# One group of heads fewer in the plain part of the fifth stage, with the first chunk's sums made behind its norm

## The chip, the cores and the metric

The kernel runs on one core of one Trainium2 chip. Its engines work side by side, each through its own list of instructions in order: TensorE (PE) multiplies matrices, VectorE (DVE) and ScalarE (ACT) work element by element, GpSimd (POOL) and SyncE (SP) mostly start transfers between the chip's buffer and the memory outside it. An engine waits where an instruction needs what another has not finished. The metric is device time in microseconds (us) from start to end of one execution. The kernel before took 2325.74 us, the median of three runs (2324.58 to 2327.02).

## What is computed

A decoder of two layers, 1024 prompt tokens and 8 sampled tokens, width 2048, all in float32. In the reference, cut to what matters here:

```python
# layer A
z = x @ w_in;  u, gate = z[..., :2048], z[..., 2048:]
d = multiscale_pool(u);  d = grouped_linear(d) * scale
h = layer_norm(ALPHA * x + (d * silu(gate)) @ w_out)
# one K and V for what follows
k, v = split(h @ w_kv);  k = rope_partial(k)
# layer B
z = h @ w_in_b;  q = rope_partial(z[..., :2048]);  gate = z[..., 2048:]
o = sliding_window_attention(q, k, v, sinks)      # 32 heads, window 128
y = layer_norm(ALPHA * h + (o * silu(gate)) @ w_out_b)
```

`layer_norm` takes mean and variance over the 2048 channels of a token. The kernel also returns the pooling state and the last keys and values.

## The kernel before, in words

**Chunks and stages.** Channels lie on the 128 partitions, tokens along a row. The tokens are cut into two chunks: chunk 0 has 512 columns, chunk 1 has 520 (512 prompt tokens and the 8 sampled ones). `PHASES` lists ten stages in order: `ai` (layer A's input product, pooling, gate), `ao` (its output product), `bi` (layer B's input product: first K and V, then queries and gates of the heads, and the attention), `bo` (its output product). Counted by kind and chunk, with a stage's two parts taken together, they are ai 0, ai 1, ao 0, ao 1, bi 0 (the fifth), bi 1, bo 0, bo 1.

**Two ways to multiply.** A weight block is 128 partitions by 1024 columns. Each float32 operand is split in a high and a low part (`cast_to` on ACT, line 502; `prep_to` on DVE, line 517), and a product is three matmuls: high by high, high by low, low by high. The plain way (`unit`, lines 709 to 711) needs four weight blocks for a two-by-two set of tiles and runs over all 512 columns. The Strassen way (`seven`, lines 681 to 683) does the same with seven products of half the columns. It needs sums of weight blocks (made on DVE, either by `plain_pair`, line 289, or by `first_pair`, line 347, and stored by POOL for the second chunk, which loads them with `next_pair`) and sums of the activation tiles: `t_ops` (lines 849 to 852) makes four sums of each pair of tiles and stores them in the tensors `Td`, from where `x_load` fetches them.

**Groups of heads.** `bi` works through eight groups p = 0 to 7, each with two query tiles and two gate tiles, so two calls of `attend`. In the plain part a group is four units; in the Strassen part it is two times seven blocks. `PHASES` says how many groups of chunk 0 are plain: `("bi", 0, (0, 3))`, that is p = 0, 1 and 2. `FORM` lists the groups whose weight sums are not made in chunk 0's plain part but in chunk 1 (`bi` 1) with `first_pair`; a plain group outside `FORM` makes and stores them on the way (`plain_pair`).

**The norms run beside the products.** `ln_gen` is a generator: each step issues a few instructions. `end()` runs at the end of each block (of each half block in the plain part) and takes a step of the first generator in the list `side` where a counter says so: one step in `every` ends, if at least `room` buffer slots are free. Extra steps are put at given ends with `at`. Before a stage's activations are first needed, `x_begin` calls `ready`, which takes at once whatever steps of the generator it depends on are left.

- In ao 1 the generator is the norm of chunk 0 (`ln_gen(0, ...)`), one step in two ends (`every = 2`). Given no `td`, its last loop takes one step a pair of tiles: subtract the mean (line 1022), multiply (1023), then on ACT the affine part of the pair before (1014) and its store by SP (1015).
- In the plain part of bi 0 the generators are the norm of chunk 1 (given `td`, so it also calls `t_ops`, two steps a pair) and behind it `t_gen(("h", 0))`, which loads chunk 0's normalised tiles again, makes their sums and stores them. One step is taken at each end, and ten extra steps at the third end and every second one from there. The Strassen part waits in `x_begin` for all of `t_gen`.
- `sum_gen("wob")` makes weight sums for `bo`. It may load while `self.on` is set: from the fourth to the twelfth end of this part, and again from the eighth of bi 1.

**Attention.** `attend` puts the scores on PE (line 1817) nine ends after the unit that makes the queries is begun. The rotated query comes from DVE (`q_done`, lines 1679 and 1787). The softmax runs on ACT and DVE over the next ends (1838, 1842), then come the transposes on PE, a masked copy on DVE (1880) and the product with the values (1894).

Program order is kept on PE, DVE and ACT (`in_order`). PE runs through its blocks; DVE and ACT prepare blocks up to three and four ahead (`self.ahead`), and loads run seven ahead (five in the plain part).

Of the kernel before, what the change touches and what calls it, by code (L numbers as in the profile page):

```python
# [43 lines left out]
C_SCALE, C_GA, C_BA, C_GB, C_BB, C_SINK, C_SDEC = 0, 16, 32, 48, 64, 80, 112  # L44
# [3 lines left out]
N_CST = K_MP + P + 1  # L48

PHASES = (  # L50
    ("ai", 0, (0, 1)), ("ai", 0, (1, 8)), ("ai", 1, (0, 8)), ("ao", 0, None), ("ao", 1, None), ("bi", 0, (0, 3)),
    ("bi", 0, (3, 8)), ("bi", 1, (0, 8)), ("bo", 0, None), ("bo", 1, None),
)
PHASE_OF = {"x": "ai", "g": "ao", "h": "bi", "o": "bo"}
INPUT_OF = {k: x for x, k in PHASE_OF.items()}
# [15 lines left out]
)  # L71

LATE = (2, 3)
FORM = (1, 2,)
X_KEEP = 5
X_AGE = 3
SIDE_KEEP = 5
# [111 lines left out]
class Kern:  # L189
# [1970 lines left out]
    def run(self):  # L2160
# [10 lines left out]
        def add(key, gen):  # L2171
            self.needs.append((key, gen))
            self.side.append(gen)

        acc, before = {}, False
        for n, (kind, c, part) in enumerate(PHASES):
            self.c, self.ph = c, kind + str(c)
            self.strassen = (kind, c, part) not in PLAIN
            self.shared = False
            self.fresh = c == 1 and before and self.strassen  # L2180
            before = c == 0 and self.strassen
            nxt = n + 1 if n + 1 < len(PHASES) else None
            self.every, self.room = 3, SIDE_KEEP
            if n == 0 or (kind, c) == ("bi", 0) and self.wide:
                self.use_four(kind == "ai")
            elif (kind, c) == ("bo", 0):
                self.at(18, lambda: self.use_four(True))

            self.lock = (kind, c) in LOCKED
            self.need = {  # L2190
                (idx, g): self.i + (2 * n + g - 1 if self.lock else n)
                for n, idx in enumerate(ORDERL if self.lock else ORDER7) for g in range(2)
            } if self.strassen else {}
            self.turn = not self.lock
            self.at(7, lambda: setattr(self, "turn", False))
            self.at(13, lambda: setattr(self, "lock", False))
            if n == 0:
                self.at(10, lambda: self.x_begin(1))
                self.at(10, lambda: setattr(self, "turn", True))
            elif (kind, c) == ("ai", 0):  # L2200
                add(("x", 1, False), self.t_gen(("x", 1)))
                self.room = 99
            elif (kind, c) == ("ai", 1):
                add(("g", 0, False), self.t_gen(("g", 0)))
                self.summed["woa"] = 0
                add("woa", self.sum_gen("woa"))
                self.every = 1.7
            elif (kind, c) == ("ao", 0):
                self.every = 2
                self.at(1, lambda: self.nc.sync.dma_start(self.cst[:, K_MP:], io["mask"]))  # L2210
            elif (kind, c) == ("ao", 1):
                gen = self.ln_gen(0, *acc[0], C_GA, C_BA, self.act["h", 0], None)
                self.at(3, lambda gen=gen: add(("h", 0, True), gen))
                self.every = 2
            elif (kind, c) == ("bi", 0) and not self.strassen:
                self.summed["wob"] = 0
                self.extra = self.sum_gen("wob")
                for k in (4, 12):
                    self.at(k, lambda k=k: setattr(self, "on", k == 4))
                add(("h", 1, False), self.ln_gen(1, *acc[1], C_GA, C_BA, self.act["h", 1], self.Td.get(("h", 1))))  # L2220
                add(("h", 0, False), self.t_gen(("h", 0)))

                for k in range(10):
                    self.at(2 * k + 3, lambda: self.side and self.lastO < self.i - 1 and self.side_step())
                self.every = 1
            elif (kind, c) == ("bi", 1):
                self.at(8, lambda: setattr(self, "on", True))
                self.every, self.room = 1, 0
            elif (kind, c) == ("bo", 0):
                self.at(23, lambda: setattr(self, "ahead", (7, 4, 3)))  # L2230
                self.at(18, lambda: add(("o", 1, False), self.t_gen(("o", 1))))
                self.at(16, lambda: [s.free() for s in self.kv])
                self.rt.free()
            elif (kind, c) == ("bo", 1):
                gen = self.ln_gen(0, *acc[0], C_GB, C_BB, io["y0"], None)
                self.at(3, lambda gen=gen: add("y", gen))
                self.every, self.room = 2.75, 3
            if kind == "ai":
                self.phase_ai(c, range(*part), nxt)
            elif kind == "bi":  # L2240
                self.phase_bi(c, range(*part), nxt)
            else:
                res = self.act["x" if kind == "ao" else "h", c]
                last = (C_GB, C_BB, io["y1"]) if nxt is None else None
                acc[c] = self.phase_out(c, res, nxt, last)
# [143 lines left out]
```

## Time and profile before

| | |
|---|---|
| median of three runs | 2325.74 us |
| the profiled execution | 2326.46 us, of which the traced span is 2324.7 us |
| PE busy | 2290.2 us (99% of the span) |
| DVE busy | 1935.0 us (83%) |
| ACT busy | 1381.8 us (59%) |
| moved by transfers | 652.50 MB, 281 GB/s on average |
| ao 1 | about 915 to 1076 us of the span |
| bi 0, plain part | 1076.45 to 1276.75 us |
| bi 0, Strassen part | from 1276.75 us |

The page gives busy time by engine, the span in 40 slices, the transfer queues, the chain that ended last and the costliest groups of instructions. A busy matmul record is longer than the distance to the next one, because matmuls are pipelined: what a stage costs PE is read from the starts of its instructions. Idle time of an engine that is not the bound costs nothing.

### The profile page before, as it was taken

Reading aid. Unit: us, or ns where it says so; the run is one execution under the profiler, and the core shown is the slowest. Engines: PE = TensorE matmul, PEld = TensorE weight load, DVE = VectorE, ACT = ScalarE, POOL = GpSimd, SP = SyncE. Lnnn points to the kernel's source line nnn. Section 1 sums busy time; section 2 is a strip of 40 time slices with the busy share of each in tenths; the row PEclk is TensorE's granted clock in tenths of the full one; section 3 lists DMA queues with packets and bytes.
Section 4 is the critical chain, followed back from the end, with each engine's and each line's share of the span. In section 5 each row is a group of like instructions: output and inputs, shape, how many; then the busy total and the mean of one; then the engine's idle time right before and its main releaser. Section 6 shows DMA issues by size and latency. Waiting matters only on the chain. (4 is left out here: it accounts for less than half of the span.)

```text
span 2324.7 us, 50174 instructions
## 1 busy us (share of the span) xinstructions
PE 2290.2 (99%) x20248; PEld 2208.9 (95%) x20248; DVE 1935.0 (83%) x2398; ACT 1381.8 (59%) x2531; POOL 191.7 (8%) x360
## 2 busy tenths in 40 slices
PE   8999999999999999999999999999999999999997
PEld 6999999999999999999778999999999999999997
DVE  7888889877878878878987888988987777898897
ACT  5554446544546556655466676785676678656565
POOL 0111110010000000000110111100000000000001
PEclk9999999999999999999999999999999999999999
DMA  6868679988889989898797667788586778799794
GB/s 247 280 252 304 234 243 333 322 299 302 303 306 317 338 284 336 321 350 310 236 349 256 220 224 254 256 306 259 178 262 225 252 233 284 254 368 363 266 345 157
DMA packets 247417, 652.50 MB, mean 281 GB/s; under 512 B 25328, under 2 KB 106128, under 8 KB 247184
## 3 DMA queue, kind: packets, MB, share of 16 engines
q1 hardware_dynamic: 205168, 496.81, 63.6%
q0 software_dynamic: 42016, 152.49, 17.0%
q8 instruction: 158, 2.59, 0.4%
q14 instruction: 75, 0.61, 0.1%
HBM read 466.68 MB, written 173.01 MB: 275 GB/s over the span
## 5 line engine op out<-in xcount | busy, mean ns | idle before, releaser
L681 PE MATMUL pD<-m,m 128*128 128x260 f32 (+1 forms) x4976 | 1408.7, 283 | 3.0 <-ACT pD L620 1.3
L683 PE MATMUL pD<-m,m 128*128 128x260 f32 (+1 forms) x4976 | 1402.2, 282 | 6.1 <-DVE m L517 5.7
L682 PE MATMUL pD<-m,m 128*128 128x260 f32 (+1 forms) x4976 | 1402.3, 282 | 0.0
L681 PEld LDWEIGHTS pD<-m,m 128*128 128x128 f32 x4976 | 936.6, 188 | 12.4 <-issue 6.0
L683 PEld LDWEIGHTS pD<-m,m 128*128 128x128 f32 x4976 | 937.7, 188 | 9.2 <-DVE m L517 9.2
L682 PEld LDWEIGHTS pD<-m,m 128*128 128x128 f32 x4976 | 937.0, 188 | 0.5
L517 DVE TENSOR_TENSOR m<-m,m 128x1024 fp32r<-128x1024 f32 x686 | 829.5, 1219 | 93.8 <-ACT m L502 53.8
L502 ACT CAST m<-m 128x1024 fp32r<-128x1024 f32 x686 | 716.9, 1050 | 237.7 <-DVE m L347 116.4
L347 DVE TENSOR_TENSOR m<-m,m 128x1024 f32<-128x1024 f32 x128 | 156.5, 1222 | 8.0 <-DMA m<-in_wia 3.8
L801 DVE TENSOR_TENSOR m<-m,m 128x1024 fp32r<-128x1024 f32 (+1 forms) x120 | 146.3, 1225 | 8.2 <-ACT m L792 4.0
L709 PE MATMUL pD<-m,m 128*128 128x512 f32 x320 | 128.7, 402 | 8.1 <-ACT m L792 8.1
L792 ACT CAST m<-m 128x1024 fp32r<-128x1024 f32 (+1 forms) x120 | 125.5, 1053 | 15.4 <-DVE m L517 4.8
L710 PE MATMUL pD<-m,m 128*128 128x512 f32 x320 | 127.2, 398 | 0.5 <-DVE m L801 0.5
L711 PE MATMUL pD<-m,m 128*128 128x512 f32 x320 | 126.8, 396 | 0.0
L654 ACT COPY m<-pD 128x260 f32<-128x260 f32 (+1 forms) x87 | 32.6, 374 | 128.8 <-PE pD L683 128.6
L642 DVE TENSOR_TENSOR m<-pD,m 128x260 f32<-128x260 f32 (+1 forms) x90 | 37.7, 419 | 76.7 <-ACT pD L641 70.8
L1853 ACT ACTIVATE m<-m,sm 128x128 f32<-128x128 f32 x256 | 99.8, 394 | 0.0
L1128 PE MATMUL pD<-m,m 128*128 128x260 f32 (+1 forms) x528 | 91.2, 323 | 0.0
L620 ACT ACTIVATE pD<-pD 128x260 f32<-128x260 f32 (+1 forms) x88 | 32.7, 371 | 98.3 <-PE pD L683 98.0
L1866 ACT ACTIVATE m<-m,sm 128x128 f32<-128x128 f32 x256 | 82.2, 394 | 12.2 <-DVE sm L1861 11.7
L1128 PEld LDWEIGHTS pD<-m,m 128*128 128x128 f32 x528 | 79.3, 188 | 8.0
L709 PEld LDWEIGHTS pD<-m,m 128*128 128x128 f32 x320 | 60.8, 190 | 23.4 <-ACT m L792 8.1
(247 smaller groups left out, 2065.0 us busy)
## 6 DMA issues: line engine op xcount, KB each, us to landing
m<-in_wia SPq DMA_DIRECT2D x130, 512.0 KB
m<-in_wib SPq DMA_DIRECT2D x130, 512.0 KB
m<-swoa SPq DMA_DIRECT2D x64, 512.0 KB
swia<-m POOLq DMA_DIRECT2D x56, 512.0 KB, 4.9
m<-swia SPq DMA_DIRECT2D x56, 512.0 KB
m<-swob SPq DMA_DIRECT2D x56, 512.0 KB
m<-in_wob SPq DMA_DIRECT2D x52, 512.0 KB
m<-in_woa SPq DMA_DIRECT2D x48, 512.0 KB
```

The source lines that it names most:

```text
L347: self.nc.vector.tensor_add(s[out].a[:, :1024], s[x].a[:, :1024], s[y].a[:, :1024])
L502: self.nc.scalar.copy(hi.r[:, :1024], self.stream[self.cast].src().a[:, :1024])
L517: self.nc.vector.tensor_sub(lo.r[:, :1024], s.src().a[:, :1024], hi.a[:, :1024])
L681: nc.tensor.matmul(ps[:, :TH], wh[:, s], h, start=new and k == 0, stop=False, skip_group_check=on)
L682: nc.tensor.matmul(ps[:, :TH], wh[:, s], l, start=False, stop=False, skip_group_check=on)
L683: nc.tensor.matmul(ps[:, :TH], wl[:, s], h, start=False, stop=k == 7, skip_group_check=on)
L709: nc.tensor.matmul(ps[:], wh[:, s], h, start=par == 0 and k == 0, stop=False)
L710: nc.tensor.matmul(ps[:], wh[:, s], l, start=False, stop=False)
L711: nc.tensor.matmul(ps[:], wl[:, s], h, start=False, stop=par == 1 and k == 7)
L792: self.nc.scalar.copy(h.r[:, :n], s.a[:, :n])
L801: self.nc.vector.tensor_sub(l.r[:, :n], s.a[:, :n], h.a[:, :n])
L1128: nc.tensor.matmul(ps[:, : cs.stop - cs.start], ws[:, s], d[:, cs], start=f0 and k == 0, stop=l0 and k == 3,)
```

## The change

It touches the plan of the stages and the pace of the work beside them.

- The plain part of bi 0 has groups 0 and 1; group 2 moves to the Strassen part. `FORM` becomes (0, 1), so both plain groups leave their weight sums to chunk 1, and group 2's sums are made in bi 0's Strassen part.
- The norm of chunk 0 in ao 1 is given `Td["h", 0]`: it makes the four sums of each pair of tiles behind the affine part and stores them from POOL. Its last loop takes two steps a pair. `every` is 1.5, two steps in three ends. `t_gen(("h", 0))`, its loads, sums, stores and the wait for it are gone from bi 0.
- The norm of chunk 1 gets fourteen extra steps in the plain part of bi 0, from the fifth end on at every second one, instead of ten from the third, and its steps no longer depend on free slots (`room = -20`).
- `sum_gen("wob")` may load at one end of that part only.

```diff
-    ("ai", 0, (0, 1)), ..., ("ao", 1, None), ("bi", 0, (0, 3)),
-    ("bi", 0, (3, 8)), ("bi", 1, (0, 8)), ("bo", 0, None), ("bo", 1, None),
+    ("ai", 0, (0, 1)), ..., ("ao", 1, None), ("bi", 0, (0, 2)),
+    ("bi", 0, (2, 8)), ("bi", 1, (0, 8)), ("bo", 0, None), ("bo", 1, None),
...
-FORM = (1, 2,)
+FORM = (0, 1)
...
             elif (kind, c) == ("ao", 1):
-                gen = self.ln_gen(0, *acc[0], C_GA, C_BA, self.act["h", 0], None)
+                gen = self.ln_gen(0, *acc[0], C_GA, C_BA, self.act["h", 0], self.Td["h", 0])
                 self.at(3, lambda gen=gen: add(("h", 0, True), gen))
-                self.every = 2
+                self.every = 1.5
             elif (kind, c) == ("bi", 0) and not self.strassen:
...
-                for k in (4, 12):
+                for k in (4, 5):
                     self.at(k, lambda k=k: setattr(self, "on", k == 4))
                 add(("h", 1, False), self.ln_gen(1, *acc[1], C_GA, C_BA, self.act["h", 1], self.Td.get(("h", 1))))
-                add(("h", 0, False), self.t_gen(("h", 0)))
-
-                for k in range(10):
-                    self.at(2 * k + 3, lambda: self.side and self.lastO < self.i - 1 and self.side_step())
-                self.every = 1
+
+                for k in range(14):
+                    self.at(2 * k + 5, lambda: self.side and self.lastO < self.i - 1 and self.side_step())
+                self.every, self.room = 1, -20
```

The loop of the norm that the changed argument switches, and the sums that it calls, are unchanged:

```python
        for p in range(10):
            load(p + 2)
            if p < 8:
                ...
            if 1 <= p <= 8:
                affine(p - 1)
                if td is None:
                    pre[p - 1].free(True)
            if td is not None:
                yield
            if p >= 2 and td is not None:
                t = self.pair_view(pre[p - 2], T)
                self.t_ops(t[:, 0], t[:, 1], td, p - 2, T // 2)
                pre[p - 2].free(True)
            yield
```

More of the change, by code (lines that the diff above doesn't have):

```diff
@@ L50 @@
 PHASES = (
-    ("ai", 0, (0, 1)), ("ai", 0, (1, 8)), ("ai", 1, (0, 8)), ("ao", 0, None), ("ao", 1, None), ("bi", 0, (0, 3)),
-    ("bi", 0, (3, 8)), ("bi", 1, (0, 8)), ("bo", 0, None), ("bo", 1, None),
+    ("ai", 0, (0, 1)), ("ai", 0, (1, 8)), ("ai", 1, (0, 8)), ("ao", 0, None), ("ao", 1, None), ("bi", 0, (0, 2)),
+    ("bi", 0, (2, 8)), ("bi", 1, (0, 8)), ("bo", 0, None), ("bo", 1, None),
 )
```

## The prediction

> **What bounds the kernel now.** I read the page first, then PE's waits, then busy time by stage, then PE's starts around the fifth stage, and last what DVE and the transfers do where work is moved to.
>
> ```profile
> span 2324.7 us, 50174 instructions
> PE 2290.2 (99%) x20248; PEld 2208.9 (95%) x20248; DVE 1935.0 (83%) x2398; ACT 1381.8 (59%) x2531; POOL 191.7 (8%) x360
> PEclk9999999999999999999999999999999999999999
> ```
>
> PE is busy all along at full clock. What it waits for, by the list of waits from 1076 to 1290 us (the fifth stage; first row) and from 1510 to 1760 us (the start of bi 1; second row), is little:
>
> ```profile
> PE pS L1817 <- DVE m L1787: 1.5, 1, 1.5
> ...
> PE pO L1894 <- DVE m L1880: 1.0, 1, 1.0
> ```
>
> So time here is PE's own work: fewer or shorter matmuls shorten the kernel, and everything else counts only where it makes PE wait. DVE is the engine that could. Stretches in the order ao 1; the fifth stage until its first scores, with them, and after them; one later stretch of its Strassen part:
>
> ```profile
> 915.00:1076.40 161.40, 160.87 (x1337) 160.29 (x1336) 132.61 (x130) 98.43 (x136) 4.94 (x11) 1.00 0.91 332
> ...
> 1076.40:1138.40 62.00, 61.50 (x273) 49.89 (x273) 53.28 (x58) 24.59 (x33) 6.31 (x11) 1.00 0.79 271
> 1138.40:1188.00 49.60, 48.14 (x326) 38.55 (x325) 48.98 (x70) 32.76 (x66) 8.11 (x16) 1.00 0.89 319
> 1188.00:1276.80 88.80, 88.80 (x644) 71.53 (x643) 66.85 (x107) 51.52 (x126) 10.39 (x21) 1.00 0.78 282
> ...
> 1342.00:1402.00 60.00, 60.00 (x699) 58.50 (x698) 53.48 (x63) 42.33 (x102) 7.61 (x15) 1.00 0.67 234
> ```
>
> After the interval come its length, then PE, weight loads, DVE, ACT, POOL busy, the granted clock, the transfers' share and GB/s. From 1138 to 1188 DVE is full (48.98 of 49.60 us), and there PE has its 1.5 us wait.
>
> **Part 1: group 2 by Strassen instead of plain.** PE's starts one period of a group apart, from the timeline: two plain (starting half a group apart, both of two attentions), two Strassen.
>
> ```profile
> 1196.74 0.39 PE L709 MATMUL pD<-m,m 128*128 128x512 f32 x1
> 1223.41 0.40 PE L709 MATMUL pD<-m,m 128*128 128x512 f32 x1
> 1250.05 0.39 PE L709 MATMUL pD<-m,m 128*128 128x512 f32 x1
> 1276.75 0.28 PE L681 MATMUL pD<-m,m 128*128 128x256 f32 x1
> 1348.38 0.28 PE L681 MATMUL pD<-m,m 128*128 128x256 f32 x1
> 1396.54 0.28 PE L681 MATMUL pD<-m,m 128*128 128x256 f32 x1
> 1444.60 0.28 PE L681 MATMUL pD<-m,m 128*128 128x256 f32 x1
> ```
>
> A plain group takes 1250.05 - 1196.74 = 53.31 and 1276.75 - 1223.41 = 53.34 us; a Strassen group 48.16 and 48.06. None of these holds a PE wait. The plain part has the same ramp at its start and the same twenty half blocks after its second `x_begin`, whether it has two groups or three, and the Strassen part the same entry; so one steady plain period goes and one steady Strassen period comes: 53.32 - 48.11 = **-5.2 us**. A check on matmuls alone: a plain half block (24 matmuls) takes 5.56 us, four Strassen blocks 11.23 us (rows below). A group is 8 of the first or 14 of the second: 44.5 - 39.3 = 5.2 again, so the attention costs about the same either way.
>
> ```profile
> 1238.05 0.39 PE L709 MATMUL pD<-m,m 128*128 128x512 f32 x1
> 1243.61 0.40 PE L709 MATMUL pD<-m,m 128*128 128x512 f32 x1
> ...
> 1330.06 0.28 PE L681 MATMUL pD<-m,m 128*128 128x256 f32 x1
> 1341.29 0.28 PE L681 MATMUL pD<-m,m 128*128 128x256 f32 x1
> ```
>
> Group 2 then costs DVE 14 subtractions and 8 weight sums and POOL 8 stores, what each Strassen group costs now at 53.48 of 60 us of DVE and no PE wait: no charge.
>
> **Part 2: the plain part's DVE.** Group 0 no longer makes its weight sums there. In that part, by groups of lines (1076 to 1277 us), and two starts of `t_gen`'s sums, four instructions apart:
>
> ```profile
> L289 DVE TENSOR_TENSOR m<-m,m 128x1024 f32<-128x1024 f32 x16 | 19.5, 1220 | 0.2
> ...
> 1217.04 0.42 DVE L849 TENSOR_TENSOR m<-m 128x256 f32<-128x256 f32 x1
> 1218.50 0.42 DVE L849 TENSOR_TENSOR m<-m 128x256 f32<-128x256 f32 x1
> ```
>
> Eight of the sixteen L289 are K's and V's and stay; eight go, 8 x 1.22 = -9.8 us before the waiting score, with their stores on POOL. (Group 2's eight come in the Strassen part; were DVE not able to cover them there, they would cost these 9.8 us.) The norm of chunk 1, at three steps in two ends for longer, has by the schedule done 45 steps by then, not 40: 5 x 1.34 (the mean of an operation of 1.22 and four sums in 1.46) = +6.7 us. DVE arrives some 3 us earlier at the rotated query, and the wait was
>
> ```profile
> 1177.88 1.32 PE L1817 MATMUL pS<-m,m 64*32 64x160 f32 x64 [1.46 <-DVE m L1787]
> ```
>
> Bounds: -1.5 (all of it goes) to +1.5 (the steps bunch and it comes twice). I take **-1.0**, nearer to the count. Next late there would be ACT, busy 32.76 of 49.60 us. `room = -20` only takes a gate away; buffers stay free since eight stored sums no longer hold them. `t_gen`'s loads (8 on SP), 32 sums (8 x 1.46 = 11.7 us of DVE) and 8 POOL stores are gone here; no PE wait hangs on them now, so 0. The norm's last steps now fall beside the loads for the Strassen part on SP's queue, where each of its stores waits for ACT with loads behind it; weights are loaded five blocks of over 5.5 us ahead there, which covers it: 0.
>
> **Part 3: ao 1 gets those 32 sums and 8 stores.** DVE in the norm's loop, and the period of seven blocks on PE:
>
> ```profile
> 987.03 2.36 DVE L517 TENSOR_TENSOR m<-m,m 128x1024 fp32r<-128x1024 f32 x2
> 989.30 1.22 DVE L1022 TENSOR_TENSOR m<-m,m 128x1024 f32<-128x1024 f32 x1
> 990.55 1.23 DVE L1023 TENSOR_TENSOR m<-m,m 128x1024 f32<-128x1024 f32 x1
> 991.70 0.42 DVE L642 TENSOR_TENSOR m<-pD,m 128x260 f32<-128x260 f32 x1
> ...
> 1001.69 0.28 PE L681 MATMUL pD<-m,m 128*128 128x260 f32 x1
> 1021.83 0.28 PE L681 MATMUL pD<-m,m 128*128 128x260 f32 x1
> ```
>
> Seven blocks last 20.14 us. In them DVE does 7 splits of 1.14 (2.27 for two), the residual's two operations at about 1.15 and two small ones at 0.42: 11.1 us. A norm pair is 1.25 + 1.15 = 2.4 us. Now it comes every two blocks, 3.5 x 2.4 = 8.4, total 19.5 of 20.14. After, every three blocks with four sums in 1.46: 7/3 x 3.86 = 9.0, total 20.1. It just fits, and has to for longer: the last pair's sums fall 37 blocks after the norm's first step, one block before `x_begin` asks for them, where now the loop ends ten blocks earlier and DVE then idles (20.25 of 34 us, below). The cover is the lead of the splits; the waits that it lets through today in this stage, and the transfers in and behind the loop:
>
> ```profile
> PE pD L683 <- DVE m L517: 0.5, 2, 0.3
> ...
> 962.00:1002.00 40.00, 40.00 (x336) 40.00 (x336) 39.52 (x38) 27.23 (x40) 1.07 (x2) 1.00 0.98 358
> 1002.00:1036.00 34.00, 34.00 (x286) 34.00 (x286) 20.25 (x20) 16.55 (x24) 0.53 (x1) 1.00 0.97 360
> ```
>
> The stores add 8 x 0.52 = 4.2 MB on POOL's queue. Nothing waits for them soon, POOL is nearly idle, and what queues behind them there are the residual's stores. SP's queue keeps its 8 stores, each waiting for ACT's affine part with the weight loads behind it, now one in three blocks instead of two. Bounds: 0 (nothing here is removed, so no gain) to 4.2 MB at 359 GB/s = +11.7 us, if transfers are the bound. I take **+0.4**, one more wait like the 0.5 us above, because the loop's rate per block hardly changes.
>
> **Part 4: bi 1.** Group 0's weight sums (8, 9.8 us of DVE) come in, group 2's go; group 1 keeps its own. DVE has idle time where the first come:
>
> ```profile
> 1561.00:1575.00 14.00, 14.00 (x135) 13.69 (x135) 8.70 (x13) 6.10 (x11) 1.29 (x2) 1.00 0.91 278
> 1575.00:1589.00 14.00, 14.00 (x119) 14.00 (x118) 13.54 (x22) 6.62 (x10) 1.26 (x2) 1.00 0.97 318
> 1589.00:1603.00 14.00, 14.00 (x119) 14.00 (x119) 6.97 (x7) 6.63 (x10) 0.73 (x1) 1.00 0.92 280
> ```
>
> 5.3 + 0.5 + 7.0 = 12.8 us idle against 9.8. Bounds: -1.0 (the wait on L1880 above, at the start of group 2, goes) to +3.7 (three sums all in the full 14 us). I take **0**. The part of the output weights' sums that moves here from the fifth stage (two loads, four additions, a store) finishes with the rest well before bo 0 loads them: 0.
>
> **Sum.** -5.2 - 1.0 + 0.4 + 0 = -5.8 us. The profiled execution took 2326.46 us (span 2324.7 and 1.8 around it), 0.7 above the median of 2325.74; so it would be 2320.7, and the median **2319.9 us**.
>
> **Rivals.**
> *The waits eat it.* The norm of chunk 1 now meets the scores of both plain groups at full pace. If the 1.5 us wait stays and comes again at the next two scores, and bi 1 adds 1 us: -5.2 + 3.0 + 0.4 + 1.0 = -0.8, 2324.9 us. For it: DVE is full from 1138 to 1188. Against it: the count of part 2.
> *Slower: ao 1 becomes bound by its transfers.* Their share is 0.97 to 0.98 from 962 to 1036 us; if none of the 4.2 MB finds room, weights come 11.7 us late in all, and 2325.74 - 5.2 + 11.7 = 2332.2 us. It turns slower than before once over 5.2 us reach PE. Against it: two slices of that stretch carry more than its mean, and after it lies room:
>
> ```profile
> 972.40:986.80 14.40, 14.40 (x122) 14.40 (x122) 14.09 (x13) 9.76 (x14) 0.53 (x1) 1.00 1.00 382
> ...
> 1001.20:1015.50 14.30, 14.30 (x122) 14.30 (x121) 9.59 (x10) 8.30 (x12) 0.00 (x0) 1.00 1.01 397
> ...
> 1044.20:1058.60 14.40, 14.40 (x123) 14.40 (x122) 8.70 (x10) 9.99 (x13) 0.06 (x1) 1.00 0.58 194
> ```
>
> The Trainium skill, page "DMA: Bandwidth & Descriptors", section "Where 436 GB/s comes from", speaks for this rival: transfers between HBM and the buffer are bound at about 358 GB/s for a core, and by that figure the 74 us at 358 to 360 GB/s are full and all of the 4.2 MB would queue. The same page calls it the share where both cores of a pair stream; the rows of 382 and 397 GB/s, on one core, lie above it, so the trace does not agree; of the 0.11 below I put 0.02 on it.
> *The norm is not ready in time.* If free slots fall under five in ao 1, steps are skipped and the rest runs at once before the fifth stage. Eight steps left are about 11 us of DVE; with two blocks (5.8 us) of lead PE waits 5: 2325.74 - 5.2 + 5 = 2325.5 us. Against it: by the schedule it ends in time, and PE has no wait there but the 0.5 us above.
>
> **How the numbers follow.** A measurement of this kernel tells about 0.2% (4.7 us) from no change: faster means under 2321.1. Chances: the forecast 0.71 (of it 0.06 with parts 2 to 4 at their dearer values and so over 2321.1), the waits 0.15, transfers 0.11 (0.02 of it milder and within 0.2%), the norm late 0.03. That gives faster 0.65, same 0.26, slower 0.09. The range runs from -5.2 - 1.5 - 1.0 = -7.7, so 2318.0, up to 2325.2, which takes in the waits; above lie transfers and half of the late norm.
>
> **What would show it.** Right: bi 0's Strassen part starts about 53 us earlier and lasts 48 longer; no L1817 wait for L1787; in ao 1 lines 849 to 852 with 32 instructions, DVE near full until about 1035 us and PE's waits for L517 under 1 us. Wrong: PE waits on L517 or L502 of several us between 960 and 1040, or between 1555 and 1620; or scores waiting for L1787 in both plain groups.

## The result, and the profile after

The changed kernel took 2320.33 us (median of nine runs, 2317.56 to 2322.83) against 2325.79 us for the kernel before beside it (nine runs): a ratio of 0.9976, 95% interval 0.9968 to 0.9985. That is 5.5 us, or 0.24%, faster; 5.8 us were forecast. The profiled execution took 2318.94 us.

Its page, span and busy time of the engines:

```profile
span 2317.2 us, 50458 instructions
...
PE 2282.8 (99%) x20392; PEld 2212.5 (95%) x20392; DVE 1942.2 (84%) x2404; ACT 1388.4 (60%) x2544; POOL 192.0 (8%) x360
```

PE is busy 7.4 us less, DVE 7.2 us more. The list of PE's waits, 1076 to 1290 us (first row) and 1510 to 1760 us:

```profile
PE pD L681 <- ACT m L2079: 1.6, 1, 1.6
...
PE pD L669 <- ACT m L654: 1.6, 1, 1.6
PE pD L681 <- ACT m L654: 0.5, 1, 0.5
```

The 1.5 us wait of the score L1817 for the rotated query is gone, and so is bi 1's 1.0 us wait of L1894. In their place stand two of 1.6 us on the entry to a stage. Where the time went is read from the starts of the stages on PE. The timeline of the kernel after, at the first matmul of the fifth stage, of its Strassen part, of bi 1 and of a block late in bi 1; then the kernel before at the last two places:

```profile
1077.20 0.39 PE L709 MATMUL pD<-m,m 128*128 128x512 f32 x1
1223.72 0.38 PE L681 MATMUL pD<-m,m 128*128 128x256 f32 x1 [1.58 <-ACT m L2079]
1514.32 0.28 PE L681 MATMUL pD<-m,m 128*128 128x260 f32 x1
1703.15 0.28 PE L681 MATMUL pD<-m,m 128*128 128x260 f32 x1
```
```profile
1076.45 0.40 PE L709 MATMUL pD<-m,m 128*128 128x512 f32 x1
1517.84 0.37 PE L681 MATMUL pD<-m,m 128*128 128x260 f32 x1
1708.84 0.28 PE L681 MATMUL pD<-m,m 128*128 128x260 f32 x1
```

| | before | after | difference |
|---|---|---|---|
| start of the fifth stage | 1076.45 | 1077.20 | +0.75 |
| plain part of bi 0 | 200.30 (1276.75 - 1076.45) | 146.52 | -53.78 |
| Strassen part of bi 0 | 241.09 (1517.84 - 1276.75) | 290.60 | +49.51 |
| bi 1 to the block shown | 191.00 | 188.83 | -2.17 |
| so at that block | 1708.84 | 1703.15 | -5.69 |

The profiled executions end 7.5 us apart; the last 2 of these come up in bo 1, whose code is the same, and the medians do not have them.

Stretches of the kernel after: two of ao 1, then the one of the fifth stage with the first scores (columns as in the prediction):

```profile
962.00:1002.00 40.00, 40.00 (x337) 40.00 (x336) 37.09 (x45) 23.48 (x34) 2.66 (x5) 1.00 0.97 346
1002.00:1036.00 34.00, 33.97 (x284) 33.76 (x283) 29.95 (x43) 19.69 (x28) 3.20 (x6) 1.00 1.02 412
1138.40:1188.00 49.60, 49.60 (x331) 39.65 (x331) 46.12 (x71) 37.54 (x78) 4.58 (x9) 1.00 0.93 329
```

From 1002 to 1036 us DVE went from 20.25 to 29.95 us and the transfers from 360 to 412 GB/s, with PE as busy as before. From 1138 to 1188 us DVE has 3.5 us to spare where it had 0.6. By groups of lines, DVE's sixteen weight sums L289 in the plain part have become eight (9.7 us), and in ao 1 there are now eight each of the four sums L849 to L852.

### The profile page after: what moved, and what is told of

Read it like the earlier page. It is cut to its first block, busy times and chain, and to the rows that moved or that the text cites. A ratio compares the mean times of both kernels' runs of the same rounds, so it can differ in the third digit from the quotient of the medians.

```text
span 2317.2 us, 50458 instructions
## 1 busy us (share of the span) xinstructions
PE 2282.8 (99%) x20392; PEld 2212.5 (95%) x20392; DVE 1942.2 (84%) x2404; ACT 1388.4 (60%) x2544; POOL 192.0 (8%) x360
## 4 chain that ended last, share of the span: by engine, by line
PE 55%; DVE 2%; ACT 1%; DMA 1%; issue 0%; SPq 0%; POOL 0%; ACTq 0%; POOLq 0%; DVEq 0%
PE pD L681 14%; PE pD L683 14%; PE pD L682 14%; PE pO L1894 2%; PE pD L709 2%; PE pD L710 2%; PE pD L711 2%; PE pS L1817 2%; PE pS L1870 1%; PE pS L1894 0%; DVE m L517 0%; DMA m<-in_wob 0%; DMA m<-m 0%; PE pO L681 0%; PE pO L683 0%
## 5 line engine op out<-in xcount | busy, mean ns | idle before, releaser
L681 PE MATMUL pD<-m,m 128*128 128x260 f32 (+1 forms) x5088 | 1440.4, 283 | 5.6 <-ACT pD L620 2.1
L683 PE MATMUL pD<-m,m 128*128 128x260 f32 (+1 forms) x5088 | 1433.1, 282 | 5.4 <-DVE m L517 5.3
L682 PE MATMUL pD<-m,m 128*128 128x260 f32 (+1 forms) x5088 | 1433.7, 282 | 0.0
L517 DVE TENSOR_TENSOR m<-m,m 128x1024 fp32r<-128x1024 f32 x692 | 836.0, 1218 | 97.7 <-ACT m L502 46.1
L502 ACT CAST m<-m 128x1024 fp32r<-128x1024 f32 x692 | 722.5, 1049 | 247.8 <-DVE m L347 118.5
L347 DVE TENSOR_TENSOR m<-m,m 128x1024 f32<-128x1024 f32 x136 | 166.2, 1222 | 8.0 <-DMA m<-in_wia 4.2
L792 ACT CAST m<-m 128x1024 fp32r<-128x1024 f32 (+1 forms) x120 | 125.5, 1052 | 11.1 <-DVE m L517 4.2
L654 ACT COPY m<-pD 128x260 f32<-128x260 f32 (+1 forms) x89 | 33.2, 373 | 131.5 <-PE pD L683 131.5
L709 PE MATMUL pD<-m,m 128*128 128x512 f32 x256 | 102.9, 402 | 8.1 <-ACT m L792 8.1
L710 PE MATMUL pD<-m,m 128*128 128x512 f32 x256 | 102.0, 399 | 0.5 <-DVE m L801 0.5
L711 PE MATMUL pD<-m,m 128*128 128x512 f32 x256 | 101.8, 398 | 0.0
L1128 PE MATMUL pD<-m,m 128*128 128x260 f32 (+1 forms) x528 | 91.2, 323 | 0.0
L629 ACT COPY m<-pD 128x260 f32<-128x260 f32 (+1 forms) x92 | 34.3, 373 | 81.1 <-PE pD L683 80.5
```

The costliest lines, as they stand in the source:

```text
L347: self.nc.vector.tensor_add(s[out].a[:, :1024], s[x].a[:, :1024], s[y].a[:, :1024])
L502: self.nc.scalar.copy(hi.r[:, :1024], self.stream[self.cast].src().a[:, :1024])
L517: self.nc.vector.tensor_sub(lo.r[:, :1024], s.src().a[:, :1024], hi.a[:, :1024])
L681: nc.tensor.matmul(ps[:, :TH], wh[:, s], h, start=new and k == 0, stop=False, skip_group_check=on)
L682: nc.tensor.matmul(ps[:, :TH], wh[:, s], l, start=False, stop=False, skip_group_check=on)
L683: nc.tensor.matmul(ps[:, :TH], wl[:, s], h, start=False, stop=k == 7, skip_group_check=on)
```

## The experiments

Each is held against the kernel before, run beside it on the same chip (2326.1 to 2326.6 us). The changed kernel stands at 0.9976 (0.9968 to 0.9985) by the same measure.

| run | what | median us | ratio, 95% interval |
|---|---|---|---|
| e1 | two groups and their `FORM` alone | 2345.64 | 1.0082 (1.0068 to 1.0096) |
| e2 | chunk 0's sums moved, nothing else | 2325.39 | 0.9997 (0.9988 to 1.0005) |
| e11 | changed, those sums left where they were | 2340.99 | 1.0062 (1.0049 to 1.0076) |
| e10 | changed, old extra steps of the norm | 2318.78 | 0.9964 (0.9952 to 0.9977) |
| e3 | changed, `FORM = (1, 2)` | 2329.41 | 1.0015 (1.0006 to 1.0024) |
| e13 | changed, group 0's sums back, no stores | 2326.49 | 1.0000 (0.9991 to 1.0009) |
| e14 | changed, group 0's stores back, no sums | 2319.77 | 0.9973 (0.9962 to 0.9983) |
| e6 | changed, ao 1's sums made twice | 2328.82 | 1.0008 (0.9999 to 1.0017) |
| e5 | changed, ao 1's sums stored twice | 2322.91 | 0.9983 (0.9974 to 0.9992) |
| e7 | changed, x tiles made earlier | 2330.26 | 1.0021 (1.0012 to 1.0030) |
| e8 | changed, one plain group | 2331.74 | 1.0026 (1.0016 to 1.0035) |
| e12 | e10, one x tile later | 2325.26 | 0.9996 (0.9987 to 1.0005) |

### e1: the groups alone

```diff
 (kernel before)
-    ("bi", 0, (0, 3)), ("bi", 0, (3, 8))
+    ("bi", 0, (0, 2)), ("bi", 0, (2, 8))
-FORM = (1, 2,)
+FORM = (0, 1)
```

> The kernel before with two plain groups and sums at the first use of groups 0 and 1 only; chunk 0's sums stay in the fifth stage and the norm of chunk 1 keeps its old pace. My theory (the gain is the group, the moved sums and the faster norm keep the waits away): by its schedule 9 norm steps and all 10 steps of the moved sums are then left when the Strassen part's x is asked for and run at once, some 24 us of DVE against about 16 us of lead, so PE gets a new wait of about 8 us there, or several that add up to it: -5.2 - 1.0 + 8, about 2327 to 2328 us. Rival (parts 2 and 3 are not needed, DVE catches up hidden): -5.2 to -6.2 us, about 2320 us, with no PE wait over 2 us at the start of the Strassen part.

PE's waits in the fifth stage of e1, and then stretches of it with the granted clock (the third number from the right): in the long wait, just behind it, and 6 us later.

```profile
PE pD L711 <- DVE m L517: 13.1, 1, 13.1
PE pS L1817 <- DVE m L1787: 3.0, 1, 3.0
```
```profile
1176.00:1184.00 8.00, 0.00 (x0) 0.00 (x0) 7.83 (x22) 0.00 (x0) 2.78 (x6) 0.50 1.03 407
1185.00:1188.00 3.00, 3.00 (x8) 2.33 (x8) 1.03 (x3) 0.00 (x0) 0.00 (x0) 0.50 1.03 409
1190.00:1191.00 1.00, 1.00 (x6) 0.84 (x5) 0.00 (x0) 0.43 (x1) 0.00 (x0) 1.00 1.02 407
```

The wait came as my theory had it, in place and by cause (DVE works through the steps left: 7.83 of 8 us), but the two waits are 16.1 us, twice what I had expected, and they cost more than their length: behind the long one the granted clock is 0.50, and PE runs at half speed for 4.2 us after it starts again, and for 3.4 us behind the second. The time is 25 us above the changed kernel; the two waits and the clock behind them make about 20. Another 3.6 us arise near 1820 us, where L1894 waits twice, 0.95 and 1.13 us, and the clock is 0.50 for 3.4 us behind that; why these two waits came was not found, nor where the rest comes from.

### e2: the move alone

```diff
 (kernel before)
-   gen = self.ln_gen(0, *acc[0], C_GA, C_BA, self.act["h", 0], None)
+   gen = self.ln_gen(0, *acc[0], C_GA, C_BA, self.act["h", 0], self.Td["h", 0])
-   self.every = 2
+   self.every = 1.5
...
-   add(("h", 0, False), self.t_gen(("h", 0)))
```

> The kernel before with chunk 0's 32 sums and 8 stores moved into the norm of the stage before (pace 1.5 there) and nothing else: three plain groups, group 0 still makes its weight sums in the fifth stage, old pace of the norm of chunk 1. My theory: the move costs about +0.4 us in the stage before and nothing else changes but 11.7 us less DVE in the fifth stage, behind the 1.5 us wait of the score L1817, which so stays: 2326 us (2325.5 to 2326.5), and the fifth stage starts about 0.4 us later than before. Rival (transfers bind there): the fifth stage starts 2 to 11.7 us later, up to 2337 us.

The list of waits of e2, fifth stage:

```profile
PE pS L1817 <- DVE m L1787: 1.3, 1, 1.3
```

The time is that of the kernel before, and the wait at L1817 is still there. From the start of one block ahead of the moved work (at 913.50, 913.08 and 913.82 us) to the fifth stage, by the timelines, the kernel before takes 162.95 us, e2 163.09 and the changed kernel 163.38: the move costs 0.1 to 0.4 us. By itself it brings nothing either.

### e11: everything but the move

```diff
 (changed kernel)
-   gen = self.ln_gen(0, *acc[0], C_GA, C_BA, self.act["h", 0], self.Td["h", 0])
+   gen = self.ln_gen(0, *acc[0], C_GA, C_BA, self.act["h", 0], None)
-   self.every = 1.5
+   self.every = 2
...
+   add(("h", 0, False), self.t_gen(("h", 0)))
```

> The changed kernel with chunk 0's 32 sums left in the fifth stage, behind the norm of chunk 1, and the stage before as it was (its norm one step in two ends). By its schedule only few norm steps, but all 10 steps of these sums (11.7 us of DVE, 8 loads, 8 stores) are left when the Strassen part's x is asked for, and they run at once. My theory (the move of the sums is what the group's removal needs): about 12 to 16 us of DVE in a lump against a lead of the splits of 10 to 14 us, so a PE gap of 3 to 8 us just before or in the last plain blocks and 2 to 3 us for the halved clock: 2325 to 2331 us. Rival (the faster pace alone is enough, the move is not needed): no gap over 2 us, 2319.5 to 2321 us.

The list of waits of e11: PE's in the fifth stage, and DVE's from 1150 to 1186 us.

```profile
PE pD L711 <- DVE m L517: 14.4, 1, 14.4
```
```profile
DVE m L849 <- DMA m<-h: 4.6, 2, 3.2
```

The lump is there and the move is what the smaller plain part needs: without it the gain of 5.5 us turns into a loss of 14.4 (2340.99 against 2326.60 beside it). The size was missed by a factor of two, for two reasons. By DVE's timeline nine steps of the norm (three multiplications L1023 and six sets of sums) run in the lump as well, not a few. And DVE idles 4.6 us in the lump, since the tiles that it is to sum come late (L849 waits for their load, transfers at 407 GB/s from 1171 to 1184 us).

### e10: the old extra steps

```diff
 (changed kernel)
-   for k in range(14):
-       self.at(2 * k + 5, ...
+   for k in range(10):
+       self.at(2 * k + 3, ...
```

> The changed kernel, but the norm of chunk 1 takes the old 10 extra steps from the third end, not 14 from the fifth; chunk 0's sums stay in the stage before. By its schedule the norm then ends at block 394, 5 blocks later than in the changed kernel, its last steps inside the Strassen part. My theory of the changed kernel (the sums that left the stage make the room, the pace matters little): PE's waits from 1076 to 1300 us stay under 3 us in all and the time is 2320 to 2322 us. Rival (the pace is what keeps the waits away): a wait of over 3.5 us of PE where the Strassen part begins, with the clock halved behind it for 4 to 6 us, 2326 us or more.

The list of waits of e10, fifth stage, has one row:

```profile
PE pD L681 <- ACT m L2079: 1.6, 1, 1.6
```

The faster pace of the norm is not needed: without the 32 sums behind it, its last steps may fall into the Strassen part. Its interval and the changed kernel's overlap, so the two are not told apart.

### e3, e13, e14: what made the wait at L1817

```diff
 (changed kernel; e3)
-FORM = (0, 1)
+FORM = (1, 2)
```

> The changed kernel, but groups 1 and 2 make weight sums at their first use, as before, not 0 and 1. My theory (group 0's 8 sums ahead of the first score cause the 1.5 us wait of the score L1817 for the addition L1787, and group 2's sums in bi 1 the slow start of its group 2): that wait is back in the fifth stage (1 to 3 us), bi 1's third group loses about 2 us again, so about +3.5 us to the changed kernel, 2323.8 us. Rival (the waits went because of the sums of chunk 0 that left the stage, or of the pace): no wait at L1817 and the time stays within 1 us of the changed kernel's 2320.3.

PE's waits in e3, in the fifth stage and in bi 1:

```profile
PE pS L1817 <- ACT m L502: 6.7, 1, 6.7
...
PE pD L669 <- ACT m L654: 2.1, 1, 2.1
PE pO L1894 <- DVE m L1880: 0.7, 1, 0.7
```

The rival falls: with group 0's sums back the wait is back, though neither of the reasons that the rival named was undone. But it is 6.7 us and not 1 to 3. The faster pace may be why it is longer than before; no run shows that alone. Two causes lie on top of each other there, DVE's load and 407 GB/s of transfers. (In bi 1 L1894 waits for L1880 again, but at the second attention; before it was at the first.) The next two runs take the two causes apart: group 0 goes through `plain_pair` again, in e13 without its stores, in e14 without its sums (those of K and V keep both).

```diff
 (changed kernel; e13, and e14 with the other of the two lines left out)
     def add1(self, s, out, a, b, dst, *free):
         def go():
             self.nc.vector.tensor_add(s[out].a[:, :1024], ...)
-            self.nc.gpsimd.dma_start(dst, s[out].a[:, :1024])
...
-   ((self.bare_pair if p in FORM else pr)("wib", q) for q in (p, 8 + p))
+   ((self.bare_pair if p == 1 else pr)("wib", q) for q in (p, 8 + p))
```

> The changed kernel with group 0's 8 weight sums made again in the plain part (9.8 us of DVE), but without their stores. What it tells apart: the run with group 0's sums back had a PE gap of 6.7 us at the score L1817, DVE full ahead of it and 407 GB/s of transfers. If DVE's count makes that gap (my theory, part 2 of the prediction): L1679 starts at about 1178 to 1180 us instead of 1170.35, PE gets a gap of 4 to 6 us at L1817 and the halved clock behind it, 2326 to 2328 us. If the transfers make it: no gap over 1.5 us, 2320 to 2321 us.

> The changed kernel with the 8 stores of group 0's weight pairs in the plain part, 4.2 MB on POOL's queue, but without the sums (the raw blocks are stored, into a place that is not read). If DVE's count makes the gap at L1817 (my theory): L1679 still starts before 1173 us, no gap over 1.5 us there, at most 1 us more than the changed kernel, 2320 to 2321.5 us. If the transfers make it: the swap of the query's halves lands late, L1679 waits for it, and PE has a gap of 3 us or more: 2325 us or more.

The rotation of the query on DVE, by the timelines of the kernel before, the changed kernel, e10, e3, e13 and e14 (line numbers are two higher in e13, one higher in e14), and the wait of e13:

```profile
1175.71 1.29 DVE L1679 TENSOR_TENSOR m<-m,m 128x512 f32<-128x512 f32 x2
```
```profile
1170.35 1.29 DVE L1679 TENSOR_TENSOR m<-m,m 128x512 f32<-128x512 f32 x2
```
```profile
1168.23 1.29 DVE L1679 TENSOR_TENSOR m<-m,m 128x512 f32<-128x512 f32 x2
```
```profile
1180.24 1.29 DVE L1679 TENSOR_TENSOR m<-m,m 128x512 f32<-128x512 f32 x2 [1.55 <-DMA m<-m]
```
```profile
1179.11 1.29 DVE L1681 TENSOR_TENSOR m<-m,m 128x512 f32<-128x512 f32 x2
...
PE pS L1819 <- DVE m L1789: 5.1, 1, 5.1
```
```profile
1169.49 1.29 DVE L1680 TENSOR_TENSOR m<-m,m 128x512 f32<-128x512 f32 x2
```

Against the changed kernel, the sums alone move the rotation by 8.8 us of the 9.8 that they take, and make a gap of 5.1 us; the stores alone do not delay it. So DVE's work is the cause. In e3 the transfers add the last 1.6 us: there the rotation waits 1.55 us for the swapped halves of the query (DMA m<-m).

### e6 and e5: what binds ao 1

```diff
 (changed kernel; e6)
-   self.t_ops(t[:, 0], t[:, 1], td, p - 2, T // 2)
+   self.t_ops(t[:, 0], t[:, 1], td, p - 2, T // 2, c == 0)    # four sums twice
 (changed kernel; e5, behind the same line)
+   if c == 0:
+       nc.gpsimd.dma_start(self.spare[:, p - 2], pre[p - 2].a[:, : 2 * T]...)
```

> The changed kernel with each of the 32 sums in ao 1 made twice (the same values again, no further transfer): 11.7 us more DVE in that stage, 3.4 us more per seven blocks that last 20.1 us. My theory (DVE just fits there, and only the lead of the splits covers more): the loop of the norm then needs about 23.5 us of DVE per seven blocks, the lead is used up, and PE waits for L517 in many small pieces, 4 to 10 us in all, before the fifth stage starts: 2324 to 2330 us. Rival (transfers set the rate there, DVE has slack): no new wait, the fifth stage starts within 0.5 us of the changed kernel's, 2320.3 us.

> The changed kernel with a second store of 512 KB behind each of the 8 new stores in ao 1, into a tensor that nobody reads: 4.2 MB more on POOL's queue, no more DVE. My theory (the transfers have room there, they went to 412 GB/s without a PE wait): the fifth stage starts 0 to 1 us later than in the changed kernel, 2320 to 2321.5 us. Rival (their bound lies at about the 412 GB/s seen in the changed kernel, so the second 4.2 MB queue): 5 to 10 us of PE waits for L517 between 960 and 1080, 2326 to 2330 us.

PE's waits in e6 in ao 1, then one stretch of e6 as above, and two of e5:

```profile
PE pD L683 <- DVE m L517: 5.9, 6, 2.9
```
```profile
1002.00:1036.00 34.00, 28.76 (x212) 28.07 (x211) 33.38 (x53) 17.02 (x24) 3.19 (x6) 0.90 0.99 366
```
```profile
962.00:1002.00 40.00, 40.00 (x336) 40.00 (x335) 37.09 (x45) 23.68 (x34) 5.32 (x10) 1.00 1.02 406
1002.00:1036.00 34.00, 31.91 (x264) 31.49 (x263) 26.08 (x36) 17.61 (x27) 4.26 (x8) 1.00 1.02 409
```

DVE is the first bound of ao 1: 11.7 us more of it cost 8.5 us, 5.9 of them in waits for L517, and some 3 in the clock behind the longest one (0.90 on average in the stretch). The transfers are the next bound, and near: with another 4.2 MB they stay at 406 to 409 GB/s there, do not pass the 412 of the changed kernel, and PE loses about 2 us from 1002 to 1036 (the medians lie 2.6 us apart, but their intervals overlap and do not show it by themselves). For e5 both expectations missed, mine by too little (0 to 1 us) and the rival by too much (5 to 10): the changed kernel uses nearly the last of this room.

### e7: x tiles earlier, for the new wait

```diff
 (changed kernel)
-   X_KEEP + {"bi0": 4, "bi1": 2, "bo0": 1}.get(self.ph, 0)
+   X_KEEP + {"bi0": 4 if self.strassen else 1, "bi1": 2, "bo0": 1}.get(self.ph, 0)
```

> The changed kernel, but in the plain part of the fifth stage the x tiles for the next part may be made with 6 slots free instead of 9. My theory: the new 1.6 us wait of PE (L681 for L2079, on entering the Strassen part) comes from x tiles held back by that rule until just before the part starts; it shrinks below 0.5 us, and the time is about 1.3 us less than the changed kernel's, 2319.0. Rival (the wait is DVE's and ACT's load at that place, whatever the order): the wait stays at 1 to 2 us or moves to a neighbouring line, and the time stays at 2320.3; fewer free slots could also make weights late, a wait of L681 for L517 of up to 3 us.

The wait in e7, and a stretch of it behind the wait:

```profile
PE pD L681 <- ACT m L2079: 4.2, 1, 4.2
```
```profile
1225.00:1230.00 5.00, 5.00 (x23) 5.00 (x24) 1.63 (x3) 2.72 (x6) 0.00 (x0) 0.50 0.51 190
```

My theory fell, and the delay does not come from the tiles' casts. The cast L502 ahead of the softmax's exponentials on ACT (1853) starts at 1211.88 us, 1.2 us later than in the changed kernel (1210.66), though e7 is 1.35 us ahead until then; from it to the copy L2079 both take the same (12.48 and 12.44 us), with one tile's cast more in between in e7. The 2.6 us are lost before that: L502 waits for DVE's sum L347, and DVE stood still at L1903, which writes the attention's output into a buffer slot taken anew (the changed kernel, then e7):

```profile
1200.19 0.69 DVE L1903 SCALAR_TENSOR_TENSOR m<-pO,m 128x512 f32<-128x512 f32 x1 [2.13 <-PE pO L1894]
```
```profile
1203.13 0.69 DVE L1903 SCALAR_TENSOR_TENSOR m<-pO,m 128x512 f32<-128x512 f32 x1 [6.41 <-PE pS L1817]
```

In e7 L1903 begins only when the next score L1817, from 1201.70 to 1203.02 us, is done with its tiles. A slot that comes free late, because the x tiles take theirs earlier, would look like this; no run shows that it is so.

The wait grew by 2.6 us, and then the first block of the Strassen part ran at half the clock (7.61 us from its start to the next, against 4.90). Another 6 us were lost at about 1802 us, by a wait of 3.3 us of L1894 and the clock behind it; why there was not found.

### e8: one plain group

```diff
 (changed kernel)
-    ("bi", 0, (0, 2)), ("bi", 0, (2, 8))
+    ("bi", 0, (0, 1)), ("bi", 0, (1, 8))
-FORM = (0, 1)
+FORM = (0,)
...
-   if t == 2 * ps[-1] - 1:
+   if t == max(2 * ps[-1] - 1, 0):
```

> The changed kernel one group further: one plain group, sums at the first use of group 0 only, the Strassen part's x asked for one block in. By its schedule the norm of chunk 1 ends 28 blocks into the Strassen part instead of 7. My theory: another 53.3 - 48.1 = 5.2 us go from PE's work, against waits of 1 to 4 us where the Strassen part begins: 2316 to 2319 us. Rival (the clump of DVE and ACT at that place grows with what the plain part no longer hides; a PE gap of over 3 us is followed by the granted clock at 0.50 for 4 to 6 us, as the runs with undone parts show): a gap of over 4 us and 2 to 3 us more for the clock, 2322 us or more.

The list of waits of e8 from 1076 to 1300 us, and a stretch behind a gap of 2.35 us at 1710:

```profile
PE pS L1817 <- DVE m L1787: 5.0, 1, 5.0
PE pD L681 <- ACT pD L641: 3.5, 1, 3.5
PE pD L681 <- ACT pD L620: 2.4, 1, 2.4
```
```profile
1713.00:1717.00 4.00, 4.00 (x97) 3.58 (x93) 4.00 (x6) 3.72 (x9) 0.56 (x1) 1.00 0.91 286
```

The rival holds. The next group takes another 5.2 us off PE's work, and e8 still ends 11.4 us above the changed kernel: three waits of 10.9 us in all, and some 6 us for the halved clock behind them. In this form the step of this change was the last that paid.

### e12: one tile later

```diff
 (e10)
-   X_KEEP + {"bi0": 4, "bi1": 2, "bo0": 1}.get(self.ph, 0)
+   X_KEEP + {"bi0": 4 if self.strassen else 5, "bi1": 2, "bo0": 1}.get(self.ph, 0)
```

> The run with the old pace, and in the plain part the x tiles are held to 10 free slots instead of 9, so that one cast of an x tile (1.03 us on ACT, the one just ahead of the copy L2079) moves behind the entry to the Strassen part. My theory: PE's 1.6 us wait of L681 for L2079 there shrinks to 0.5 to 1.0 us, nothing else changes, and the time is some 0.6 to 1.1 us under the run with the old pace: 2317.9 us. Rival (the tile is then late itself, or the tile's cast is not what L2079 waits behind): the wait stays at 1.6 us, or L681 waits for L801 within the next blocks, 2318.8 us or more.

The lists of waits of e12, from 1076 to 1300 us (first row) and from 1780 to 1830; the cast of an x tile ahead of L2079 in e12; then a cast of a weight block on ACT near 1795 in e10 and in e12:

```profile
PE pD L681 <- ACT m L2079: 1.7, 1, 1.7
...
PE pO L1894 <- DVE m L1880: 1.2, 1, 1.2
PE pO L1894 <- ACT m L1879: 1.0, 1, 1.0
```
```profile
1222.60 1.04 ACT L792 CAST m<-m 128x1024 fp32r<-128x1024 f32 x1
```
```profile
1792.08 1.05 ACT L502 CAST m<-m 128x1024 fp32r<-128x1024 f32 x1 [2.44 <-DMA m<-in_wib]
```
```profile
1795.96 1.05 ACT L502 CAST m<-m 128x1024 fp32r<-128x1024 f32 x1 [4.67 <-DMA m<-in_wib]
```

The edit did not do what I had meant: both runs have eight casts L792 ahead of the entry, one moved from 1199 to 1216 us, and one still stands right ahead of the copy L2079 (1223.53). So the run does not test that tile; what the entry's wait does go with stands under part 1 below. The time rose by 6.5 us for a reason far from the edit: from about 1790 us on a weight block lands later, ACT stands still for it, and L1894 waits behind. Of 6.9 us between the two profiles, 2.5 come in this place and 2.4 at about 2030 us. That an edit at 1220 us reaches that far is measured; how (the edit changes which buffer slots later blocks get) is only a guess.

## Why the prediction was right, and where it was not

The forecast was 2319.9 us in 2318.0 to 2325.2; it came to 2320.33. Two small waits of the kernel before come into the count, by its list of waits in the plain part (first row) and on the entry to bi 1. Then follow ACT's copy out of the last plain unit, before and after, and the rotation of bi 1's first query on DVE, before and in e2:

```profile
PE pS L1741 <- ACT m L2066: 0.5, 1, 0.5
...
PE pD L669 <- ACT m L654: 0.5, 1, 0.5
```
```profile
1277.87 0.57 ACT L2079 COPY m<-pD 128x512 f32<-128x512 f32 x1
```
```profile
1223.10 0.58 ACT L2079 COPY m<-pD 128x512 f32<-128x512 f32 x1
```
```profile
1601.87 2.39 DVE L1679 TENSOR_TENSOR m<-m,m 128x1040 f32<-128x1040 f32 x2 [3.57 <-DMA m<-m]
```
```profile
1599.50 2.39 DVE L1679 TENSOR_TENSOR m<-m,m 128x1040 f32<-128x1040 f32 x2 [0.61 <-DMA m<-m]
```

By the prediction's steps:

- **Part 1, -5.2 us: right, but for the entry.** Before, one steady plain period less and one steady Strassen period more were -53.32 and +48.11. The plain part became 53.78 us shorter: 53.32, plus the 1.46 and the 0.5 us waits that went, less the 1.58 us wait that came, make 53.70. The Strassen part became 49.51 longer: 48.11 and the 1.2 us that the entry to bi 1 waits longer (1.63 us at L669, 0.46 before; the lists round) make 49.3. What failed is the clause "and the Strassen part the same entry", and ACT's load is not what changed there. Before, the copy L2079 comes 1.12 us behind the first Strassen matmul (1276.75), and PE does not wait for it. After, it comes 0.96 us behind the time at which PE stops (1222.14), and PE waits. The buffer differs: plain units take three buffers `pD` for their products in turn (line 241), Strassen blocks take theirs by a switch (lines 603 and 604). Followed through the code, the first Strassen block begins in buffer 1 in both kernels, and the last plain unit sits in buffer 2 with three groups but in buffer 1 with two, so that it has to be copied out first. With one group it is buffer 0. The runs fit: all with two groups have this wait, those with three (before, e2) or one (e8, where the copy comes 7.8 us behind) do not. No run changes the buffer alone.
- **Part 2, -1.0 us: the wait went for the reason given; of the two terms of the count one held.** The wait at L1817 is gone, all 1.46 us of it, and e13 shows that the eight sums alone bring a wait there back. Their term held: 9.8 us of sums moved the rotated query by 8.8. The term of the faster pace, 6.7 us, did not. With it the query was to come some 3 us earlier; counted from the stage's start it comes 6.1 us earlier (99.26 us before, 93.15 after), and with the old pace 91.40 (e10), so that the pace costs 1.8 us. The step also counted only DVE; in this stretch the transfers rose too, to 329 GB/s (319 before), and in e3 they added 1.6 us.
- **`t_gen` gone, 0 us: right for the kernel before, and hiding the most important point.** No wait hung on it there with three groups (e2: no change). With two groups a wait of 14.4 us hangs on it, some 20 us of time (e11). The move is not a gain of its own but the condition for part 1, and the sum by parts could not show that, since each part was priced against the kernel before.
- **Part 3, +0.4 us: right,** +0.43 in the changed kernel and +0.1 in e2. The reason was right too: the loop "just fits", with a little more room than counted (DVE is idle for 4 of the 34 us behind 1002), and when its sums are doubled PE loses 8.5 us. The rival of the transfers did not come, but was closer than its 0.11 says: at 406 to 412 GB/s they are full there (e5). The Trainium skill, page "DMA: Bandwidth & Descriptors", section "Where 436 GB/s comes from", gives about 358 GB/s for transfers between HBM and the buffer; on this one core the trace holds 412 GB/s over 34 us and does not agree.
- **Part 4, 0 us: short of it, and for another reason than its lower bound had.** bi 1 is 2.2 us shorter from its first block on, but its entry waits 1.2 us longer (the term just counted with the Strassen part; its cause was not looked for), so the stage brings about -1.0 in all, the lower bound given. But it is not group 2's sums that made the difference. e2 and e3 keep them in bi 1, and from the first to the third scores L1817 of bi 1 they take 45.9 and 46.0 us, the changed kernel 45.95, the kernel before 48.49. In the profile of the kernel before, DVE waits 3.57 us ahead of these scores for the transfer that brings the swapped halves of the query (0.61 us in e2, 0.41 in e3, none in the changed kernel) and is full for the 20 us behind them. Why that transfer came late is open, and only one execution of the kernel before shows it. What goes with group 2's sums is a wait of L1894 at the second attention, 0.7 us in e3 and 0.4 in e2.

The measured terms, -5.2, -0.4 (waits of the plain part, 1.58 - 1.46 - 0.5), +0.4 and -1.0, make -6.2 us; the timelines show -6.0 from ao 1 on (-5.69, where +0.33 stood ahead of ao 1 already), the medians -5.5 in all. The new wait on the entry took most of what the waits of the plain part had given, part 4 brought a gain that the forecast had no reason for, and they cancelled. That the sum came within 0.5 us is in part luck; the group, the move and the sums of group 0 are not. Two pieces of the change, `room = -20` and the shorter time in which `sum_gen` may load, were run in no experiment by themselves.

Of the rivals, "the waits eat it" is what e3, e7 and e13 became, at 2326 to 2330 us rather than 2324.9: it was priced without the clock.

## What a wait of PE costs beside its length

I had not expected this one. In the profiles of these runs some gaps of PE are followed by a granted clock of 0.50, at which PE does about half the work (in e7 three matmuls of the first Strassen block take 0.64 us, and 0.35 once the clock is back). One of the shortest, in e5 on the entry to bi 1 (where each line number is one higher), and the stretch behind it:

```profile
1518.15 0.51 PE L670 MATMUL pD<-m,m 128*128 128x260 f32 x2 [1.76 <-ACT m L655]
```
```profile
1519.60:1522.90 3.30, 3.30 (x18) 3.30 (x17) 3.00 (x3) 3.12 (x11) 0.00 (x0) 0.50 1.06 387
```

By the timelines and the granted clock, the start and the end of the program left aside:

| gap of PE, us | run | clock 0.50 after PE's restart, us |
|---|---|---|
| 1.6 | changed kernel, entry of the Strassen part | none |
| 1.75 | e14, at 2093 | none |
| 1.76 | e5, entry of bi 1 | 3.4 |
| 1.84 | e8, at 355 | 3.4 |
| 1.92 | e1, at 355 | 3.4 |
| 0.95 and 1.13, 1.6 apart | e1, at 1820 | 3.4 |
| 2.1 | e3, entry of bi 1 | none |
| 2.35 | e8, at 1710 | none |
| 2.39 | e13, at 2101 | none |
| 2.4 | e8, at 1241 | 3.4 |
| 2.9 | e6, in ao 1 | 6.1 |
| 3.0 | e1, behind the long one | 3.4 |
| 3.3 | e7, at 1802 | 5.8 |
| 3.5 | e8, at 1197 | 5.7 |
| 4.2 | e7, entry of the Strassen part | 6.1 |
| 5.0 | e8, score L1817 | 2.9 |
| 5.1 | e13, score L1817 | 4.0 |
| 6.7 | e3, score L1817 | 4.0 |
| 13.1 | e1 | 4.2 |
| 14.4 | e11 | 4.3 |

All gaps of 2.4 us (2.43) and more in these runs are followed by the half clock, and no single gap of up to 1.75 us is. In between both happen, so the length alone does not decide; what else does is not shown. Part of the half clock can lie in the gap, and behind the shorter gaps it begins only 0.3 to 1.5 us after PE has restarted. With the part in the gap it lasts one, two or four times 3.41 us each time. What it costs is half of the last column, 1.5 to 3 us, beside the gap's length.

So e7's wait, 2.6 us longer than the changed kernel's, costs 5.3 us. The Trainium skill, page "TensorE: Matmul & The Clock Gate", section "HAM oscillation — how this bites in real kernels", warns of idle gaps of PE above about 3.4 us. The half clock agrees; the length does not: here gaps of 1.8 to 3.3 us were enough.

## What to carry to other kernels

Price an edit in the company of the others too: a move that is worth nothing by itself may be what keeps another one's gain, and the time of a lump of work left over at a stage's end (14.4 us here) shows only when the stage is made shorter. Where PE has no slack, count the work of the engine that feeds it instruction by instruction up to the place where it is needed: for work put back alone that count held to a microsecond, for steps taken at a faster pace it did not (6.7 us counted, 1.8 measured), and two edits meant to move one engine's work out of another's way (e7, e12) did something else. When a stage gets longer or shorter by a few units of work, look which buffer its last unit leaves full: that can be the one that the next stage begins with. And keep PE's gaps short: up to 1.75 us a single one cost its length here, from 2.4 us on 1.5 to 3 us more, and in between it can be either.
